# Small SBUF tiles of a diffusion-trunk kernel widened to whole 512-byte lines

## The chip, the cores and the metric

The kernel runs on one core of a Trainium2 chip. The number that counts is the device time of one execution in microseconds (us); several executions are timed and the median is taken. One more execution is recorded by the hardware profiler, and all that is said of single instructions comes from that one.

A core has a tensor engine (PE) that multiplies matrices, a vector engine (DVE), a scalar engine (ACT), GpSimd (POOL), a queue engine that issues most transfers (SP), and 16 DMA engines. The on-chip memory SBUF has 128 partitions; a tile occupies the same range of bytes in every partition. A matrix product has two operands in SBUF. The *stationary* one (here 128 columns, 512 bytes in each partition) is loaded into the array by an instruction of its own, which the profile lists as PEld. The *moving* one (here mostly 512 columns, 2048 bytes in each partition) is then streamed past it, and the sums land in PSUM. In the profile's names, `out<-moving,stationary`.

## What is computed

Two layers of a trunk over 256 latent and 256 context tokens of width 1024, in float32. Layer 0 is a convolution module, layer 1 a retention over chunks; each is followed by a gated feed-forward net of hidden width 2816, and each sub-layer is normalised and modulated by vectors made from a condition.

```python
for i in range(DEPTH):                      # DEPTH = 2
    sh_m, sc_m, g_m, sh_f, sc_f, g_f = adaln(c, ada_w[i], ada_b[i])
    hx = modulate(x, norm_mix[i], sh_m, sc_m)
    ...
    ox = conv_module(...) if i == 0 else retention_mixer(...)
    x = x + g_m * ox
    x = x + g_f * swiglu_ffn(modulate(x, norm_ffn[i], sh_f, sc_f), ffn_w_gu[i], ffn_w_down[i])
    if not last:                            # the context passes through layer 0 alone
        h_ctx = h_ctx + cg_m * oc
        h_ctx = h_ctx + cg_f * swiglu_ffn(modulate(h_ctx, ...), ffn_w_gu[i], ffn_w_down[i])
return x
```

## The kernel before

**Products in three passes.** Every large product is made by `mm3` (L188 to L192). Each operand is split into a high part and a low part of a 32-bit format that the tensor engine takes in one pass, and `hi*hi`, `hi*lo` and `lo*hi` are summed in PSUM. So all large products are runs of matmuls on lines L190, L191 and L192, 128 stationary columns by 512 (in a few places 256) moving columns. There are 4392 of them: 3912 with 512 moving columns and 480 with 256.

**Weights.** `load` (L141) brings 1 MB of weights by DMA into a `raw` tile, `split_hi` (L146) makes the high part on ACT (L153), `split_lo` (L157) the low part on DVE or POOL (L161). Three `raw` tiles and four pairs `wh`/`wl` take turns, so that loads and splits run ahead of the products.

**Stages in order of time.** Up to about 230 us: the modulation vectors of layer 0 (`ada`), the pointwise products of the convolution (`a`, `g` with `w1a`, `w1b` as stationary operand), the depthwise convolution, whose input takes a way through DRAM (`y` to `yd` to `z4`), and the last product `w`. 230 to 600 us: the feed-forward net of layer 0, up (`fa`, `fb`) and down (`dn`, `dnl`), while DVE works out the modulation of layer 1 (L850). 600 to 905 us: retention by heads (`qk`, `kc`, `v`, `sc`, `g` with `wg`, `o`, `wo`). From 905 us: the feed-forward net of layer 1, up (`u`) and down (`y`). The order of most instructions is pinned by hand; a scheduler orders the rest from a cost model.

**Which operand is which.** In `a`, `g` (w1b), `fa`, `fb` and `kc` the moving operand is the activation and the stationary one the weight. In `w`, `dn`, `dnl`, `qk`, `v`, `g` (wg), `wo`, `u` and `y` it is the other way round. In `o` the moving operand is the values and the stationary one the scores.

**Where tiles lie.** Pools are laid one behind the other in SBUF, and in a pool each tile follows the one declared ahead of it; the size in a partition is rounded up to 32 bytes and to nothing larger. The first tile starts at byte 16,512. Adding up the declared sizes gives the start of each tile, and so its remainder to 512 bytes. `cp` takes 21,440 bytes (among them `sm` with 1728, `cst` with 1168, `res`, the `mods` and `modA` tiles, `csil`, and `ab1` with 32), so that the weights and all that follows begin at 37,952 = 74 x 512 + 64. The small tiles of `sp` (`ss`, `rs_a`, `rstd`, `rs_h`, `rs_t`, two of 32 bytes each) add 320 bytes, `gcs` adds 2 x 64, and the tiles `lg` and `t8` of `rt` add 160.

| tiles (pool) | what they are to the tensor engine | start, remainder to 512, before |
|---|---|---|
| `wh`, `wl` (`wp`) | all split weights | 64 |
| `ah`, `al` (`pA`): `h0`, `z`, `hid`, `oT` | activations of `a`, `g`, `w`, `dn`, `wo` | 64 |
| `ah`, `al` (`pB`): `h0f`, `h1`, `h1f` | activations of `fa`, `fb`, `qk`, `v`, `kc`, `g`, `u` | 0 |
| `kT`, `qT`, `vh`, `vl` (`rt`); `hidT` in `kT`'s place | `sc`, values of `o`, activations of `y`, a few weights | 160 |
| `k4` (`sp`): `Ph`, `Pl` | scores of `o` | 384 |
| `idle` in `z4`'s place (`cv`) | both operands of the opening matmuls | 0 |
| `cst`, `csil` | identity and mean columns; the condition | 384; 32 |

All slices that the large products take out of these tiles begin at whole multiples of 512 bytes, so the remainder of the tile is that of every operand. Sorted by (moving, stationary), the 3912 wide ones are: (0, 64) `fa`, `fb`; (64, 0) `u`, `v`, `qk`, `g` with `wg`; (64, 160) `y`; (160, other) `o` and 48 matmuls with weights in `vh` and `vl`; (64, 64) `a`, `g` with `w1`, `w`, `dn`, `dnl`, `wo`.

Of the kernel before, what the change touches and what calls it, by code (L numbers as in the profile page):

```python
# [8 lines left out]
F32 = mybir.dt.float32  # L9
# [6 lines left out]
P = 128  # L16
D = 1024
KC = D // P
# [10 lines left out]
CST_W = 292  # L29
# [29 lines left out]
Z4 = 2  # L59
WSPLIT = 4  # L60
K4 = 5
YW = TOK + 2 * PAD
# [21 lines left out]
def trunk_kernel(ctx: ExitStack, tc, x_in, ctx_in, cond, small, consts, rope, dist, ada, adat,  # L84
# [3 lines left out]
    cp = ctx.enter_context(tc.tile_pool(name="cp", bufs=1))  # L88
    wp = ctx.enter_context(tc.tile_pool(name="wp", bufs=3))
    pA = ctx.enter_context(tc.tile_pool(name="pA", bufs=1))  # L90
    sp = ctx.enter_context(tc.tile_pool(name="sp", bufs=2))
# [3 lines left out]
    cv = cvs.enter_context(tc.tile_pool(name="cv", bufs=1))  # L95
# [4 lines left out]
    def aux(name):  # L100
        return ps.tile([P, 512], F32, tag="aux", name=name, bufs=2)
# [7 lines left out]
    nc.scalar.activation(tabl, one, AF.Silu)  # L109
    sm = cp.tile([P, SMALL_W], F32, name="sm")  # L110
    nc.scalar.dma_start(sm[:, 0:SMALL_1], small[:, 0:SMALL_1])
    cst = cp.tile([P, CST_W], F32, name="cst")
    nc.scalar.dma_start(cst, consts)
    ident = cst[:, 0:128]
    sel = cst[:, 128:130]
# [4 lines left out]
    def smc(n):  # L120
        a, b = _SM[n]
        return sm[:, a:b]
# [6 lines left out]

    load_tokens(x_in, 0)  # L130

    mods = [cp.tile([P, 48, 2], F32, name=f"mods{l}") for l in range(2)]
    modA = [[cp.tile([P, KC, 2], F32, name=f"modA{l}{j}") for j in range(2)] for l in range(2)]
    ab = smc("ab").rearrange("p (l c) -> p l c", l=2)
    ng = smc("ng").rearrange("p (l c) -> p l c", l=4)

    csil = cp.tile([P, KC, 32], F32, name="csil")
    nc.gpsimd.memset(csil, 0.0)


# [53 lines left out]
    def rsqrt(a, y, n, also=lambda i: None):  # L194


        nh = sp.tile([P, n], F32, tag="rs_h", name="rs_h")
        tt = sp.tile([P, n], F32, tag="rs_t", name="rs_t")
        also(nc.vector.tensor_scalar(y.bitcast(I32), a.bitcast(I32), -0.5, 1597463007.0, op0=ALU.mult, op1=ALU.add))
        also(nc.vector.tensor_scalar(nh, a, -0.5, None, op0=ALU.mult))  # L200
        for _ in range(3):
            for i in range(n):
                yi, ti = y[:, i:i + 1], tt[:, i:i + 1]
                also(nc.vector.tensor_scalar(ti, yi, yi, nh[:, i:i + 1], op0=ALU.mult, op1=ALU.mult))
            for i in range(n):
                yi, ti = y[:, i:i + 1], tt[:, i:i + 1]
                also(nc.vector.tensor_scalar(yi, ti, 1.5, yi, op0=ALU.add, op1=ALU.mult))

    def halves(t):
        return [t[:, 1024 * hf:1024 * hf + 1024].rearrange("p (k c) -> p k c", c=256) for hf in range(2)]  # L210
# [59 lines left out]
    def gate_to_rows(l, j, also=lambda i: None):  # L270

        c = 16 if j == 0 else 40
        pt = aux(f"gr{l}{j}")
        cs = sp.tile([P, 2, KC], F32, tag="gcs", name="gcs")
        also(nc.scalar.activation(cs, mods[l][:, c:c + KC, :].rearrange("p c s -> p s c"), AF.Copy))
        also(nc.tensor.transpose(pt[0:16, 0:P], cs.rearrange("p s c -> p (s c)"), ident))
        sb = sp.tile([16, P], F32, tag="grow", name="grow")
        also(nc.scalar.activation(sb, pt[0:16, 0:P], AF.Copy))
        d = dr.tile([2, D], F32, name=f"grd{l}{j}")
        also(nc.sync.dma_start(d.rearrange("s (c p) -> (s c) p", p=P), sb))  # L280
        gate_rows[l, j] = d
# [7 lines left out]
    def normed(tiles, xt=None, also=lambda i: None):  # L289

        n = len(tiles)
        outs = [xt[:, i, :] if xt is not None else sp.tile([P, D], F32, tag="k4", name="xn", bufs=K4)
                for i in range(n)]
        ss = sp.tile([P, n], F32, tag="ss", name="ss")
        for i, t in enumerate(tiles):
            also(nc.scalar.activation(outs[i], res[:, t, :], AF.Square, accum_out=ss[:, i:i + 1]))
        a = sp.tile([P, n], F32, tag="rs_a", name="rs_a")
        rstd = sp.tile([P, n], F32, tag="rstd", name="rstd")
        also(nc.vector.tensor_scalar(a, ss, 1.0 / D, EPS, op0=ALU.mult, op1=ALU.add))
        rsqrt(a, rstd, n, also)  # L300
        for i, t in enumerate(tiles):
            also(nc.vector.tensor_scalar(outs[i], res[:, t, :], rstd[:, i:i + 1], None, op0=ALU.mult))
        return outs
# [5 lines left out]
    def t2(name):  # L309
        return sp.tile([P, 512], F32, tag="t2", name=name, bufs=T2)  # L310
# [106 lines left out]
    start_loads("a0 w0 a1 w1 a2 w2")  # L417
    pin(nc.sync.dma_start(sm[:, SMALL_1:], small[:, SMALL_1:]))

    idle = cv.tile([P, 4, 2 * YW], F32, tag="z4", name="idle", bufs=Z4).rearrange("p q t -> p (q t)")[:, 0:512]  # L420
    nc.gpsimd.memset(idle, 0.0)
    pw_ = acc("idle")

# [4 lines left out]
    keep_busy(START_IDLE)  # L428
    xs = normed([0, 1], xn4[:, 0:2, :], pin)
    pin(nc.scalar.activation(csil[:, :, 0:2], smc("cT").rearrange("p (k c) -> p k c", c=2), AF.Silu))  # L430
    ab1 = cp.tile([P, KC], F32, name="ab1")
    pin(nc.vector.tensor_scalar(ab1, ab[:, 0, KC:2 * KC], 1.0, None, op0=ALU.add))
    xs += normed([2, 3], xn4[:, 2:4, :], pin)
    start_T(0, (0, 1))
# [30 lines left out]
        return sg.rearrange("p (s t) -> p s t", s=2)  # L465

    def glu(ch, pa, sg):
        y = cv.tile([P, 2, YW], F32, tag="y", name="y", bufs=4)
        nc.gpsimd.memset(y[:, :, 0:PAD], 0.0)
        nc.gpsimd.memset(y[:, :, PAD + TOK:], 0.0)  # L470
        yv = y[:, :, PAD:PAD + TOK]
        av = pa.rearrange("p (s t) -> p s t", s=2)
        if ch in GLU_DVE:
            pin(nc.vector.scalar_tensor_tensor(yv, av, b1[:, ch:ch + 1], sg, op0=ALU.add, op1=ALU.mult))
        else:
            pin(nc.scalar.activation(yv, av, AF.Identity, bias=b1[:, ch:ch + 1]))
            pin(nc.gpsimd.tensor_tensor(yv, yv, sg, op=ALU.mult))
        return y
# [7 lines left out]
    def bounce_in(ch, yd):  # L486

        n = GROUPS[ch]
        dg = cv.tile([P, MAXG, 4, 32], F32, tag="dg", name="dg", bufs=2)
        pin(nc.sync.dma_start(dg[:, :n], dwd[:, ch, :n]))  # L490
        z4 = cv.tile([P, 4, 2 * YW], F32, tag="z4", name="z4", bufs=Z4)
        w = 2 * YW - 3
        for s in range(4):
            pin(nc.sync.dma_start(z4[32 * s:32 * s + 32, :, 0:w], yd[:, :, s:s + w].rearrange("q c t -> c q t")))
        return z4, dg
# [134 lines left out]
    for step in range(KC):  # L630
        d = step - 1
        c = max(step - 2, 0) if step > 1 else None
# [23 lines left out]
        if step < KC - 1:  # L656
            ys[step] = glu(step, pa, sg)
            if step == 0:
                w1_hi(K_PAIRS + 1)
            if step:  # L660
                w1_load(step + W1_AHEAD)
            if step > 1 and step + 2 < KC:
                w1_hi(step + 2)
            zs4[step] = bounce_in(step, bounce_out(step, ys[step]))
# [24 lines left out]
        if step >= KC - 3:  # L689
            i = 2 * (step - KC + 3)  # L690
            square(i)
            square(i + 1)
        if step == KC - 1:
            split_w2(0, 0, None, pin)
            ys[step] = glu(step, pa, sg)
            pin(nc.scalar.activation(tabl, one, AF.Silu))
            zs4[step] = bounce_in(step, bounce_out(step, ys[step]))

    c, d = KC - 2, KC - 1
# [14 lines left out]
    for i in range(12, 16):  # L714
        t = fills[(i - 12) // 2][:, 2048 * (i % 2):2048 * (i % 2) + 2048]
# [1 line left out]
        ada_raws[i] = halves(t)  # L717
    w2r[0, 1] = load(w2[0, 1], name="w2_01", also=pin)
    for i in (16, 17):
        t = cv.tile([P, 4, 2 * YW], F32, tag="z4", name=f"raw_ada{i}", bufs=Z4).rearrange("p q t -> p (q t)")[:, 0:2048]  # L720
        pin(nc.sync.dma_start(t, ada[ADA_PE.index(i)]))
        ada_raws[i] = halves(t)
    cols(8)
# [37 lines left out]
    cols(13)  # L761
    finish(13)
    gate_to_rows(0, 0, pin)
    gates = [gate_bc(0, 0, 0, pin), gate_bc(0, 0, 1, pin)]
    ada_raws[18] = ada_load(18, pin)
# [143 lines left out]
    for gi, (j0, gn) in enumerate(groups):  # L909
        hid = new_act(pA, f"hid{gi}")  # L910
        for j in range(j0, j0 + gn):
# [14 lines left out]
            for j, w, pa, pb in early:  # L926
                sa = t2("sa")
                nc.scalar.activation(sa, pa, AF.Silu)
                t = t2("hidt")
# [3 lines left out]
        if gates is None:  # L933
            gate_to_rows(0, 1)
            gates = [gate_bc(0, 1, 0), gate_bc(0, 1, 1)]
# [45 lines left out]
    rt = ctx.enter_context(tc.tile_pool(name="rt", bufs=1))  # L981
    Wd = pA.tile([P, HEADS, 4, TOK], F32, tag="al", name="Wd")
    dec = smc("dec")
    lg = rt.tile([P, 8], F32, name="lg")

    def decay_logs():
        t8 = [rt.tile([P, 8], F32, name=f"t8_{i}") for i in range(4)]
# [78 lines left out]
    for hd in range(HEADS):  # L1066
# [5 lines left out]
        if hd == 0:  # L1072
            w = [kview(weights(wqk[0, kh], name=f"qk0{kh}", eng=nc.gpsimd if kh in QK_POOL else None), 512) for kh in range(2)]
            for kh in range(2):
                parts = norm_parts(1, 0, 1, x1, h, TOK, pin, pin if PIN_SPLIT else (lambda i: None)) if kh else None
                proj_half(qk_x, w[kh], kh, parts)
            for _ in parts:
                pass
            gate_to_rows(1, 0)
            gate_to_rows(1, 1)  # L1080
            qn = rope_q(pq, pin)
            for kh in range(2):
                keys_c(pk, w[kh], kh)
        else:
            for kh in range(2):
                w = kview(weights(wqk[hd, kh], name=f"qk{hd}{kh}"), 512)
                proj_half(qk_x, w, kh)
                keys_c(pk, w, kh)
# [358 lines left out]
```

## Time and profile before

| | us |
|---|---|
| median of 3 timed runs | 1097.86 |
| lowest and highest of them | 1094.61 and 1098.99 |
| the profiled execution | 1095.0 |
| its span, first to last instruction | 1093.2 |

The profiled execution lies 2.9 us below the median of the three runs and inside their spread. Outside its span lie 1.8 us.

How to read it: the profile's page gives busy time by engine and the chain of work that ended last; the timeline gives the start of every instruction. The duration that the timeline shows for a matmul includes its way through the array, which overlaps with the next one. What a matmul costs in a stream is therefore the time from one start to the next, and that is called its *pitch* below. It is taken from the first and the last row of a stretch without interruption, divided by the number of starts between them.

### The profile page before, as it was taken

How to read it: one execution, taken by the hardware profiler on the slowest of the kernel's cores; microseconds unless marked ns; L12 is line 12 of the kernel's file. 1: busy time of each engine (PE TensorE's matmuls, PEld its weight loads, DVE VectorE, ACT ScalarE, POOL GpSimd, SP SyncE). 2: the span in 40 equal slices, each digit the busy share in tenths (PEclk: the TensorE clock that was granted, in tenths of full speed). 3: DMA queues.
4: the chain of work that ended last, by engine and by line, in shares of the span. 5: the costliest groups of instructions: out<-in, count | busy, mean ns of one | idle time of the engine just before them, and what ended most of it. 6: DMA issues, size and time to landing. Idle time of an engine off the chain costs nothing.

```text
span 1093.2 us, 13554 instructions
## 1 busy us (share of the span) xinstructions
PE 1068.4 (98%) x5348; PEld 845.6 (77%) x5348; DVE 688.3 (63%) x1129; ACT 414.6 (38%) x596; POOL 162.2 (15%) x121
## 2 busy tenths in 40 slices
PE   8989998999999999999999999999999989999998
PEld 4756645788888888888888788888888867888886
DVE  5598765568999885536555786457454555555445
ACT  4564544353221222212322573323332454444442
POOL 0086743030000000000000420000000461000000
PEclk9999999999999999999999999999999999999999
DMA  9489778723556676523222442235233344455551
GB/s 375 178 231 274 233 195 349 264 78 116 211 213 243 258 269 231 172 98 133 98 81 112 158 152 92 101 135 178 92 116 116 116 161 166 167 181 191 192 187 45
DMA packets 34895, 190.15 MB, mean 174 GB/s; under 512 B 3920, under 2 KB 4624, under 8 KB 15504
## 3 DMA queue, kind: packets, MB, share of 16 engines
q1 hardware_dynamic: 34400, 188.01, 48.8%
q10 hardware_dynamic: 432, 1.28, 0.4%
q8 instruction: 42, 0.69, 0.3%
q14 instruction: 21, 0.17, 0.1%
HBM read 185.85 MB, written 3.42 MB: 173 GB/s over the span
## 4 chain that ended last, share of the span: by engine, by line
PE 88%; DMA 3%; DVE 3%; ACT 2%; issue 1%; POOL 1%; SPq 0%; ACTq 0%; POOLq 0%; DVEq 0%
PE fa L191 4%; PE fa L192 4%; PE fb L191 4%; PE fb L192 4%; PE fa L190 4%; PE fb L190 4%; PE u L190 3%; PE u L192 3%; PE u L191 3%; PE v L191 3%; PE v L192 3%; PE v L190 3%; PE dn L191 3%; PE dn L192 3%; PE dn L190 3%; PE g L192 2%
## 5 line engine op out<-in xcount | busy, mean ns | idle before, releaser
L161 DVE TENSOR_TENSOR wl_gu<-raw_gu,wh_gu 128x1024 fp32r<-128x1024 f32 x76 | 92.2, 1223 | 82.3 <-ACT wh_gu L153 81.4
L153 ACT ACTIVATE wh_gu<-raw_gu 128x1024 fp32r<-128x1024 f32 x84 | 88.0, 1058 | 139.6 <-PE fb L191 52.6
L850 DVE SCALAR_TENSOR_TENSOR junk<-raw_adat,crow 128x1024 f32<-128x1024 f32 x80 | 97.6, 1220 | 0.9
L161 DVE TENSOR_TENSOR wl_dn<-raw_dn,wh_dn 128x1024 fp32r<-128x1024 f32 x38 | 46.5, 1224 | 45.4 <-ACT wh_dn L153 45.1
L190 PE MATMUL fa<-ah_h0f,wh_gu 128*128 128x512 f32 (+1 forms) x192 | 72.0, 376 | 1.0 <-DVE ah_h0f L314 1.0
L191 PE MATMUL fa<-al_h0f,wh_gu 128*128 128x512 f32 (+1 forms) x192 | 72.3, 377 | 0.0
L190 PE MATMUL fb<-ah_h0f,wh_gu 128*128 128x512 f32 (+1 forms) x192 | 72.2, 376 | 0.0
L191 PE MATMUL fb<-al_h0f,wh_gu 128*128 128x512 f32 (+1 forms) x192 | 72.0, 375 | 0.0
L192 PE MATMUL fb<-ah_h0f,wl_gu 128*128 128x512 f32 (+1 forms) x192 | 72.0, 375 | 0.0
L192 PE MATMUL fa<-ah_h0f,wl_gu 128*128 128x512 f32 (+1 forms) x192 | 72.0, 375 | 0.0
L153 ACT ACTIVATE wh_dn<-raw_dn 128x1024 fp32r<-128x1024 f32 x38 | 40.3, 1060 | 80.3 <-PE dn L192 35.5
L190 PE MATMUL u<-wh_gu,ah_h1f 128*128 128x512 f32 x160 | 63.5, 397 | 0.0
L161 POOL TENSOR_TENSOR wl_qk<-raw_qk,wh_qk 128x1024 fp32r<-128x1024 f32 x4 | 9.6, 2398 | 362.7 <-DVE res L345 350.2
L191 PE MATMUL u<-wl_gu,ah_h1f 128*128 128x512 f32 x160 | 62.6, 392 | 0.0
L192 PE MATMUL u<-wh_gu,al_h1f 128*128 128x512 f32 x160 | 62.4, 391 | 0.0
L520 POOL TENSOR_TENSOR pacc<-pacc,pr 128x512 f32<-128x512 f32 x39 | 58.7, 1506 | 15.8 <-ACT pr L519 13.4
L537 DVE SCALAR_TENSOR_TENSOR lacc<-y,sm,lacc 128x512 f32<-128x512 f32 x65 | 49.1, 755 | 2.1
L191 PE MATMUL v<-wl_v,ah_h 128*128 128x512 f32 x128 | 50.4, 393 | 0.0
L192 PE MATMUL v<-wh_v,al_h 128*128 128x512 f32 x128 | 50.1, 391 | 0.0
L190 PE MATMUL dn<-wh_dn,ah_hid 128*128 128x512 f32 x128 | 49.9, 390 | 0.0
L191 PE MATMUL dn<-wl_dn,ah_hid 128*128 128x512 f32 x128 | 49.8, 389 | 0.0
L192 PE MATMUL dn<-wh_dn,al_hid 128*128 128x512 f32 x128 | 49.8, 389 | 0.0
(309 smaller groups left out, 2653.0 us busy)
## 6 DMA issues: line engine op xcount, KB each, us to landing
raw_gu<-in_gu_dram SPq DMA_DIRECT2D x44, 1024.0 KB, 4.8
raw_adat<-in_adat_dram SPq DMA_DIRECT2D x28, 1024.0 KB, 4.8
raw_dn<-in_dn_dram SPq DMA_DIRECT2D x19, 1024.0 KB, 4.7
raw_ada<-in_ada_dram SPq DMA_DIRECT2D x13, 1024.0 KB, 9.2
z<-yd SPq DMA_DIRECT2D x32, 284.5 KB, 4.8
raw_qk<-in_wqk_dram SPq DMA_DIRECT2D x8, 1024.0 KB, 4.8
raw_v<-in_wv_dram SPq DMA_DIRECT2D x8, 1024.0 KB, 4.8
raw_g<-in_wg_dram SPq DMA_DIRECT2D x8, 1024.0 KB, 4.8
```

Of the source, the lines that this page charges most:

```text
L153: also(nc.scalar.activation(hi[:, :m], raw[:, c:c + m], AF.Copy))
L161: also((eng or nc.vector).tensor_tensor(lo[:, :m], raw[:, c:c + m], hi[:, :m].bitcast(F32), op=ALU.subtract))
L190: also(nc.tensor.matmul(o, a[0], b[0], start=first, stop=False))
L191: also(nc.tensor.matmul(o, a[0], b[1], start=False, stop=False))
L192: also(nc.tensor.matmul(o, a[1], b[0], start=False, stop=last))
L520: pin(nc.gpsimd.tensor_tensor(pacc, pacc, pr, op=ALU.add))
L537: pin(nc.vector.scalar_tensor_tensor(cacc, a, w, cacc, op0=ALU.mult, op1=ALU.add))
L850: pin(nc.vector.scalar_tensor_tensor(junk, raw[:, c, :], 1.0, crow[:, s, :], op0=ALU.mult, op1=ALU.mult, accum_out=mods[l][:, c0 + c, s:s ...
```

## The change

No instruction is added, removed or changed in shape. Some small tiles are declared wider and then cut to the part in use, and some are declared at an earlier place.

```diff
+    mods = [cp.tile([P, 48, 2], F32, name=f"mods{l}") for l in range(2)]
+    modA = [[cp.tile([P, KC, 2], F32, name=f"modA{l}{j}") for j in range(2)] for l in range(2)]
+
+    ab1 = cp.tile([P, 32], F32, name="ab1")[:, 0:KC]
+    csil = cp.tile([P, KC, 32], F32, name="csil")
-    cst = cp.tile([P, CST_W], F32, name="cst")
+    cst = cp.tile([P, 384], F32, name="cst")[:, 0:CST_W]
...
-        tt = sp.tile([P, n], F32, tag="rs_t", name="rs_t")
+        tt = sp.tile([P, 32], F32, tag="rs_t", name="rs_t")[:, 0:n]
...
-        cs = sp.tile([P, 2, KC], F32, tag="gcs", name="gcs")
+        cs = sp.tile([P, 64], F32, tag="gcs", name="gcs")[:, 0:2 * KC].rearrange("p (s c) -> p s c", s=2)
...
-    idle = cv.tile([P, 4, 2 * YW], F32, tag="z4", name="idle", bufs=Z4).rearrange("p q t -> p (q t)")[:, 0:512]
+    idle = cv.tile([P, 2304], F32, tag="z4", name="idle", bufs=Z4)[:, 0:512]
...
-        y = cv.tile([P, 2, YW], F32, tag="y", name="y", bufs=4)
+        y = cv.tile([P, 576], F32, tag="y", name="y", bufs=4)[:, 0:2 * YW].rearrange("p (s t) -> p s t", s=2)
...
-        z4 = cv.tile([P, 4, 2 * YW], F32, tag="z4", name="z4", bufs=Z4)
+        z4 = cv.tile([P, 2304], F32, tag="z4", name="z4", bufs=Z4)[:, 0:8 * YW].rearrange("p (q t) -> p q t", q=4)
...
-        t = cv.tile([P, 4, 2 * YW], F32, tag="z4", name=f"raw_ada{i}", bufs=Z4).rearrange("p q t -> p (q t)")[:, 0:2048]
+        t = cv.tile([P, 2304], F32, tag="z4", name=f"raw_ada{i}", bufs=Z4)[:, 0:2048]
...
-    lg = rt.tile([P, 8], F32, name="lg")
+    lg = rt.tile([P, 96], F32, name="lg")[:, 0:8]
```

Added up in the same way, `cp` takes 21,888 bytes, so that the weights begin at 38,400 = 75 x 512; the small tiles of `sp` take 512 bytes, `gcs` 2 x 256, `lg` and `t8` together 512. Every tile of the table above then begins at a multiple of 512, `cst` and `csil` too, and `k4`. The pool of the convolution ends 1152 bytes later than before, and all still fits. Inside `z4` the rows of 2288 bytes stay as they were, and of the four `y` tiles (2304 bytes each) two begin in the middle of a line.

More of the change, by code (lines that the diff above doesn't have):

```diff
@@ L130, in trunk_kernel @@
     load_tokens(x_in, 0)
-    mods = [cp.tile([P, 48, 2], F32, name=f"mods{l}") for l in range(2)]
-    modA = [[cp.tile([P, KC, 2], F32, name=f"modA{l}{j}") for j in range(2)] for l in range(2)]
     ab = smc("ab").rearrange("p (l c) -> p l c", l=2)
     ng = smc("ng").rearrange("p (l c) -> p l c", l=4)
-    csil = cp.tile([P, KC, 32], F32, name="csil")
     nc.gpsimd.memset(csil, 0.0)
@@ L430, in trunk_kernel @@
     pin(nc.scalar.activation(csil[:, :, 0:2], smc("cT").rearrange("p (k c) -> p k c", c=2), AF.Silu))
-    ab1 = cp.tile([P, KC], F32, name="ab1")
     pin(nc.vector.tensor_scalar(ab1, ab[:, 0, KC:2 * KC], 1.0, None, op0=ALU.add))
```

## The prediction

> **What bounds the kernel now.** The page comes first: busy time by engine, granted clock, and the chain that ended last.
>
> ```profile
> span 1093.2 us, 13554 instructions
> ...
> PE 1068.4 (98%) x5348; PEld 845.6 (77%) x5348; DVE 688.3 (63%) x1129; ACT 414.6 (38%) x596; POOL 162.2 (15%) x121
> ...
> PEclk9999999999999999999999999999999999999999
> ...
> PE 88%; DMA 3%; DVE 3%; ACT 2%; issue 1%; POOL 1%; SPq 0%; ACTq 0%; POOLq 0%; DVEq 0%
> ```
>
> PE is busy for 98% of the span at full clock, and 88% of the chain is its own work. The busy time by stretches says where.
>
> ```profile
> 230.00:600.00 370.00, 368.10 (x1699) 302.40 (x1698) 258.27 (x449) 96.48 (x116) 9.35 (x4) 1.00 0.47 171
> 600.00:905.00 305.00, 299.33 (x1492) 250.08 (x1492) 180.22 (x318) 128.77 (x184) 59.85 (x29) 1.00 0.36 130
> 905.00:1084.00 179.00, 178.46 (x800) 144.62 (x799) 90.31 (x99) 76.69 (x101) 1.50 (x1) 1.00 0.45 162
> ```
>
> The columns are the length, then PE, PEld, DVE, ACT and POOL busy with their instructions, clock and DMA. From 230 us on PE has 8.1 us without work in 854 us, and DVE, the next engine, is busy for 70% at most. So a nanosecond less between two matmuls is nearly a nanosecond less in the time, once for each.
>
> The third view is the timeline of PE. Here are the first and the last row of one stretch in each family; between the rows lie 56, 24, 18, 12, 5 and 5 starts.
>
> ```profile
> 469.83 0.39 PE L191 MATMUL dn<-wl_dn,ah_hid 128*128 128x512 f32 x1
> ...
> 482.52 0.39 PE L190 MATMUL dn<-wh_dn,ah_hid 128*128 128x512 f32 x1
> ```
> ```profile
> 425.78 0.39 PE L190 MATMUL fa<-ah_h0f,wh_gu 128*128 128x512 f32 x1
> ...
> 431.38 0.39 PE L190 MATMUL fb<-ah_h0f,wh_gu 128*128 128x512 f32 x1
> ```
> ```profile
> 87.68 0.39 PE L190 MATMUL g<-ah_h,wh_w1b 128*128 128x512 f32 x1
> ...
> 91.77 0.39 PE L190 MATMUL g<-ah_h,wh_w1b 128*128 128x512 f32 x1
> ```
> ```profile
> 980.82 0.39 PE L190 MATMUL u<-wh_gu,ah_h1f 128*128 128x512 f32 x1
> ...
> 983.57 0.39 PE L190 MATMUL u<-wh_gu,ah_h1f 128*128 128x512 f32 x1
> ```
> ```profile
> 978.49 0.40 PE L190 MATMUL y<-wh_dn,hidT 128*128 128x512 f32 x1
> ...
> 979.66 0.40 PE L192 MATMUL y<-wh_dn,hidT 128*128 128x512 f32 x1
> ```
> ```profile
> 667.00 0.40 PE L192 MATMUL o<-vh,Pl 128*128 128x512 f32 x1
> ...
> 668.16 0.39 PE L192 MATMUL o<-vh,Pl 128*128 128x512 f32 x1
> ```
>
> The pitch of one and the same form is 226.6 ns in `dn` (12.69 us / 56), 233.3 in `fa` (5.60 / 24), 227.2 in `g` with w1b (4.09 / 18), 229.2 in `u` (2.75 / 12), 234 in `y` (1.17 / 5) and 232 in `o` (1.16 / 5). What sets these apart? Not the role of the operands: `g` and `fa` both stream activations past weights, with 227.2 and 233.3. Not the stage: `dn` and `fa` take turns in the same 370 us. The table of starts fits: 227 where both operands have the remainder 64, more wherever the two differ: 229 at (64, 0), 233 at (0, 64), 234 at (64, 160), 232 at (160, 384).
>
> **The change part by part.** The program stays the same instruction for instruction; all that moves is addresses. So the sum is one of pitches times counts. After the change every large product has (0, 0), a pair that no wide one has now. I take it that two operands with the same remainder run at the pitch of `dn`, 226.6, since (64, 64) is the one alike pair that the trace has at this width.
>
> The counts, one line of three for each family (three passes, so three times as many; `qk`, `g`, `dnl`, `wo` follow from the loops):
>
> ```profile
> L190 PE MATMUL u<-wh_gu,ah_h1f 128*128 128x512 f32 x160 | 63.5, 397 | 0.0
> L191 PE MATMUL fa<-al_h0f,wh_gu 128*128 128x512 f32 x160 | 63.1, 394 | 0.0
> L190 PE MATMUL fb<-ah_h0f,wh_gu 128*128 128x512 f32 x160 | 63.1, 394 | 0.0
> L190 PE MATMUL v<-wh_v,ah_h 128*128 128x512 f32 x128 | 49.6, 390 | 0.0
> L190 PE MATMUL y<-wh_dn,hidT 128*128 128x512 f32 x88 | 33.1, 396 | 0.0
> L190 PE MATMUL o<-vh,Ph 128*128 128x512 f32 x32 | 12.6, 395 | 0.0
> ```
>
> *`fa`, `fb`:* 960 x (233.3 - 226.6) = 6.4 us. *`u`, `v`, `qk`, `g` with wg:* 1272 x (229.2 - 226.6) = 3.3 us at most. These stages are broken up by transposes. An alike stream needs a few matmuls after such a break: in `wo`, also (64, 64), the ten starts below take 2.29 us, 229 each.
>
> ```profile
> 737.04 0.39 PE L191 MATMUL wo<-wl_wo,oT 128*128 128x512 f32 x1
> ...
> 739.33 0.39 PE L192 MATMUL wo<-wh_wo,oT 128*128 128x512 f32 x1
> ```
>
> So I take 1272 x 1.6 = 2.0 us (the bounds are 0, if all behave like this stretch, and 3.3). *`y`:* 264 x (234 - 227.5) = 1.7 us. *`o` and the 48 with weights in `vh`, `vl`:* 144 x (232 - 227) = 0.7 us. The gross gain is 10.8 us.
>
> The 480 matmuls with 256 columns may lose. The one alike pair among them is `sc`, (160, 160); `fa` and `fb` of the first two blocks have (0, 64). Between these rows lie 18 and 12 starts.
>
> ```profile
> 656.62 0.28 PE L190 MATMUL sc<-qT,kT 128*128 128x256 f32 x1
> ...
> 658.78 0.28 PE L190 MATMUL sc<-qT,kT 128*128 128x256 f32 x1
> ```
> ```profile
> 239.58 0.28 PE L190 MATMUL fa<-ah_h0f,wh_gu 128*128 128x256 f32 x1
> ...
> 240.94 0.28 PE L190 MATMUL fa<-ah_h0f,wh_gu 128*128 128x256 f32 x1
> ```
>
> `sc` has 120 ns, `fa` 113.3 at its best. `sc` and `dn` together say that 256 more columns cost 226.6 - 120 = 106.6 ns, so 512 stream in 213.2, and an alike matmul adds 13.4 at either width (`fa`: 20.1 at 512, but 6.7 at 256). The bounds are 384 x 6.7 = 2.6 us lost (`kc` and `fa`/`fb` all go from 113.3 to 120) and 96 x 6.7 = 0.6 us gained (`sc` goes to 113.3). I take 1.7 us lost, two thirds of the way to the upper end, because `sc` is the only row with an alike pair.
>
> The other engines see moved addresses too. The nearest rows set two remainders side by side:
>
> ```profile
> L850 DVE SCALAR_TENSOR_TENSOR junk<-raw_adat,crow 128x1024 f32<-128x1024 f32 x80 | 97.6, 1220 | 0.9
> L161 DVE TENSOR_TENSOR wl_gu<-raw_gu,wh_gu 128x1024 fp32r<-128x1024 f32 x76 | 92.2, 1223 | 82.3 <-ACT wh_gu L153 81.4
> ...
> raw_gu<-in_gu_dram SPq DMA_DIRECT2D x44, 1024.0 KB, 4.8
> raw_adat<-in_adat_dram SPq DMA_DIRECT2D x28, 1024.0 KB, 4.8
> ```
>
> `raw_adat`, `crow` and `junk` begin at remainder 0, `raw_gu` and `wh_gu` at 64; DVE takes 1220 and 1223 ns and the transfer lands after 4.8 us in both. I count DVE, ACT, POOL and DMA at nothing. Nothing hides them at the bounce `y` to `yd` to `z4`, but the rows there keep their 2288 bytes. The single-pass products of the first 230 us (`ada`, depthwise `cv`, transposes) I also count at nothing, with 1 us to either side.
>
> One stretch of the chain is not PE's:
>
> ```profile
> 871.75 4.77 POOL wo301vl L161 x2
> 876.53 4.65 DMA raw_gu<-in_gu_dram
> ```
>
> From 870 to 905 us a faster PE only waits longer for these; the 48 matmuls with weights in `vh` and `vl` lie there and save nothing: 48 x 5 ns, 0.3 us with their neighbours. What is late next is DVE in 300 to 400 us, where it also makes the modulation of layer 1; the row of 230 to 600 us (258 of 370 busy) leaves room for 3%. **Sum:** 10.8 - 1.7 - 0.3 = 8.8 us. From the profiled execution's 1095.0 that makes 1086.2; the median of the runs lies 2.9 us higher, so **1089**.
>
> **The rivals.** The whole is 3912 x (pitch after - mean pitch now), and the mean now is 230.1 ns (960 x 233.3, 1272 x 229.2, 1272 x 227.5, 264 x 234, 144 x 232).
>
> *Slower: a moving operand at remainder 0 is what costs.* `fa`, `fb` are the only wide family that has it, and among the slowest. Then all go to 233.3: 3912 x 3.2 = 12.5 us more, 1110. It decides from 230.1 ns on. Against it: `fa` with 256 columns also moves from 0 and adds only 6.7 ns, half of `sc`; and the opening matmuls on `idle` have (0, 0).
>
> ```profile
> 7.24 4.03 PE L426 MATMUL idle<-idle 128*128 128x512 f32 x9
> ```
> ```profile
> L426 PE MATMUL idle<-idle 128*128 128x512 f32 x7 | 3.2, 593 | 0.0
> ```
>
> Nine of them end 4.03 us after the first start, so the pitch is (4.03 - 0.59) / 8 = 430 ns; that is twice 213.2 and 3 ns. They stream at half the rate, so this is a hint, not a proof.
>
> *Little or nothing.* Either (0, 0) behaves like (64, 0): 3912 x (229.2 - 230.1) is 3.5 us less, and 1.7 come back at 256 columns: 1096. Or the remainder is not the cause: 1098. For this speaks only that the pairs coincide with families; `dn` beside `fa` and `g` beside `fa` speak against. The Trainium skill, TensorE: Matmul & The Clock Gate, section "Step-by-step: what each phase is for", states that PE reads its two operands through independent ports and that a load of the next weights takes nothing from the running matmul; by that rule placement could not matter and the time would stay. The rows from 226.6 to 234 do not agree with it.
>
> *Much faster: the 13.4 ns go as well.* If what `idle` shows holds at full rate, the pitch is 216: 3912 x 14 = 55 us less, 1043. Against it: `dn` at 226.6 and `sc` at 120 are alike already and pay 13.4. The Trainium skill, TensorE: Matmul & The Clock Gate, section "Wait — 56ns, not 53.3ns?", gives 215.7 ns for 512 columns back to back; by it the gain would be 56 us, an estimate from that page. The rows of `dn` do not agree with it.
>
> **How the numbers follow.** Alike pairs as with (64, 64): 0.66, between 1083 and 1094, from the ends of the terms (gross 8.8 to 12.5, loss 2.6 to gain 0.6, 1 us for the start, and the spread of the runs). Little or nothing: 0.17. Slower: 0.13. Much faster: 0.04. Such runs can tell about 0.5%, 5.5 us, from no change. Of the first case a tenth falls within that: faster 0.62 + 0.04 = 0.66; within 0.5% 0.20; slower 0.14, with a little from the scatter of the others. The range 1081 to 1100 takes in the first two cases and leaves the two outer ones out.
>
> **What would show it.** Right: `fa`, `y`, `u` and `dn` all show one pitch near 227 in the timeline, the stretch 230 to 600 us is 6 us shorter and the start up to 230 us keeps its length. Wrong: `dn` goes up to 229 or 233 (the remainder itself counts, not the likeness), or `fa` stays at 233. If the pitches fall and the time does not, DVE or a load has become the wait, which PE's busy share would tell.

## The result, and the profile after

| | before | after |
|---|---|---|
| median of 4 timed runs, us | 1096.65 | 1086.38 |
| lowest and highest, us | 1094.61, 1098.99 | 1085.50, 1087.92 |
| the profiled execution, us (its span) | 1095.0 (1093.2) | 1087.21 (1085.4) |

The ratio is 0.9907, with a 95% interval of 0.9881 to 0.9934: the changed kernel is 0.9% faster, 10.3 us by the medians. PE, DVE, ACT and POOL have the same instructions in the same order in both traces (the one more that the page counts below belongs to the sequencer of POOL and is not counted as busy). In the changed kernel the three lines of `mm3` are L192 to L194, and later lines move down by one or two.

The page of the changed kernel: span, busy time, the granted clock in 40 slices, and the chain.

```profile
span 1085.4 us, 13555 instructions
...
PE 1062.3 (98%) x5348; PEld 851.1 (78%) x5348; DVE 687.8 (63%) x1129; ACT 414.9 (38%) x596; POOL 162.1 (15%) x121
...
PEclk8999999999999999999999999999999999999999
...
PE 91%; DVE 3%; DMA 2%; ACT 2%; issue 1%; SPq 0%; POOL 0%; ACTq 0%; DVEq 0%; POOLq 0%
```

PE is as much the bound as before. It is busy for 6.1 us less, and the span is 7.8 us shorter. DVE, ACT and POOL keep their time, and so do the rows that stood for moved addresses:

```profile
L163 DVE TENSOR_TENSOR wl_gu<-raw_gu,wh_gu 128x1024 fp32r<-128x1024 f32 x76 | 92.2, 1223 | 78.6 <-ACT wh_gu L155 77.8
...
L851 DVE SCALAR_TENSOR_TENSOR junk<-raw_adat,crow 128x1024 f32<-128x1024 f32 x80 | 97.7, 1221 | 0.9
...
raw_gu<-in_gu_dram SPq DMA_DIRECT2D x44, 1024.0 KB, 4.7
raw_adat<-in_adat_dram SPq DMA_DIRECT2D x28, 1024.0 KB, 4.8
```

Where the time went is read from the same instructions in both traces. The view of one tile gives, for each line, the count, the shortest, median and longest duration in ns, and the first and last start in us. Before:

```profile
L190 PE MATMUL fa<-ah_h0f,wh_gu x192: 276/394/398, 231.1 to 563.8; 128*128 128x512 f32 x160, 128*128 128x256 f32 x32
L192 PE MATMUL dnl<-wh_dn_l,al_hid x48: 389/389/400, 570.6 to 605.7; 128*128 128x512 f32 x48
L192 PE MATMUL wo<-wh_wo,oT x56: 387/389/398, 724.0 to 894.7; 128*128 128x512 f32 x56
L190 PE MATMUL y<-wh_dn,hidT x88: 391/394/481, 919.4 to 1087.4; 128*128 128x512 f32 x88
```

After:

```profile
L192 PE MATMUL fa<-ah_h0f,wh_gu x192: 277/389/396, 232.6 to 559.9; 128*128 128x512 f32 x160, 128*128 128x256 f32 x32
L194 PE MATMUL dnl<-wh_dn_l,al_hid x48: 389/389/397, 566.4 to 601.5; 128*128 128x512 f32 x48
L194 PE MATMUL wo<-wh_wo,oT x56: 388/390/397, 719.4 to 889.0; 128*128 128x512 f32 x56
L192 PE MATMUL y<-wh_dn,hidT x88: 389/390/477, 914.4 to 1080.0; 128*128 128x512 f32 x88
```

The first `fa` starts 1.5 us *later* than before (232.6 against 231.1). The last `dnl` starts 4.2 us earlier, so the feed-forward net of layer 0 gained 5.7 us. By the last `wo` the lead is 5.7 us (1.5 more), by the first `y` 5.0, and by the last `y` 7.4 (2.4 more). The two places where the lead shrinks, before 231 us and between 889 and 914 us, hold stretches at half clock, shown in the last section.

The pitches, from the timeline of PE after, first and last row of a stretch. From the first row to the last it is 48 starts (`dn`), 23 (`fa`), 46 (`u`), 13 (`y`), 23 (`o`) and 24 (256 columns):

```profile
457.18 0.39 PE L192 MATMUL dn<-wh_dn,ah_hid 128*128 128x512 f32 x1
...
468.06 0.39 PE L192 MATMUL dn<-wh_dn,ah_hid 128*128 128x512 f32 x1
```
```profile
272.06 0.39 PE L192 MATMUL fa<-ah_h0f,wh_gu 128*128 128x512 f32 x1
...
277.28 0.39 PE L194 MATMUL fa<-ah_h0f,wl_gu 128*128 128x512 f32 x1
```
```profile
957.62 0.39 PE L193 MATMUL u<-wl_gu,ah_h1f 128*128 128x512 f32 x1
...
968.07 0.39 PE L194 MATMUL u<-wh_gu,al_h1f 128*128 128x512 f32 x1
```
```profile
934.64 0.39 PE L192 MATMUL y<-wh_dn,hidT 128*128 128x512 f32 x1
...
937.59 0.39 PE L193 MATMUL y<-wl_dn,hidT 128*128 128x512 f32 x1
```
```profile
858.77 0.39 PE L192 MATMUL o<-vh,Ph 128*128 128x512 f32 x1
...
863.98 0.39 PE L194 MATMUL o<-vh,Pl 128*128 128x512 f32 x1
```
```profile
240.96 0.28 PE L194 MATMUL fb<-ah_h0f,wl_gu 128*128 128x256 f32 x1
...
243.84 0.28 PE L194 MATMUL fa<-ah_h0f,wl_gu 128*128 128x256 f32 x1
```

`dn` has 226.7 ns (10.88 us / 48), `fa` 227 (5.22 / 23), `u` 227.2 (10.45 / 46), `y` 226.9 (2.95 / 13), `o` 226.5 (5.21 / 23). The families that lay between 226.6 and 234 ns now share one pitch. `fa` with 256 columns went the other way, from 113.3 to 120 (2.88 / 24).

### The profile page after: what moved, and what is told of

Read it like the earlier page. It is cut to its first block, busy times and chain, and to the rows that moved or that the text cites. A ratio compares the mean times of both kernels' runs of the same rounds, so it can differ in the third digit from the quotient of the medians.

```text
span 1085.4 us, 13555 instructions
## 1 busy us (share of the span) xinstructions
PE 1062.3 (98%) x5348; PEld 851.1 (78%) x5348; DVE 687.8 (63%) x1129; ACT 414.9 (38%) x596; POOL 162.1 (15%) x121
## 3 DMA queue, kind: packets, MB, share of 16 engines
HBM read 185.85 MB, written 3.42 MB: 174 GB/s over the span
## 4 chain that ended last, share of the span: by engine, by line
PE 91%; DVE 3%; DMA 2%; ACT 2%; issue 1%; SPq 0%; POOL 0%; ACTq 0%; DVEq 0%; POOLq 0%
PE u L194 4%; PE fa L193 4%; PE u L193 4%; PE u L192 4%; PE fa L194 4%; PE fb L194 4%; PE fa L192 4%; PE fb L193 4%; PE fb L192 4%; PE v L193 3%; PE v L192 3%; PE dn L192 3%; PE dn L194 3%; PE v L194 3%; PE dn L193 3%; PE g L192 2%
## 5 line engine op out<-in xcount | busy, mean ns | idle before, releaser
L192 PE MATMUL fa<-ah_h0f,wh_gu 128*128 128x512 f32 (+1 forms) x192 | 71.4, 373 | 1.0 <-DVE ah_h0f L316 1.0
L192 PE MATMUL fb<-ah_h0f,wh_gu 128*128 128x512 f32 (+1 forms) x192 | 71.5, 373 | 0.0
L194 PE MATMUL fb<-ah_h0f,wl_gu 128*128 128x512 f32 (+1 forms) x192 | 71.4, 372 | 0.0
L194 PE MATMUL fa<-ah_h0f,wl_gu 128*128 128x512 f32 (+1 forms) x192 | 71.3, 372 | 0.0
L192 PE MATMUL u<-wh_gu,ah_h1f 128*128 128x512 f32 x160 | 63.1, 394 | 0.0
L194 PE MATMUL u<-wh_gu,al_h1f 128*128 128x512 f32 x160 | 62.3, 391 | 0.0
L521 POOL TENSOR_TENSOR pacc<-pacc,pr 128x512 f32<-128x512 f32 x39 | 58.7, 1505 | 15.7 <-ACT pr L520 13.4
L192 PE MATMUL dn<-wh_dn,ah_hid 128*128 128x512 f32 x128 | 49.9, 390 | 0.0
L194 PE MATMUL v<-wh_v,al_h 128*128 128x512 f32 x128 | 49.9, 390 | 0.0
L194 PE MATMUL dn<-wh_dn,al_hid 128*128 128x512 f32 x128 | 49.8, 389 | 0.0
```

Source lines behind the costliest of these rows:

```text
L192: also(nc.tensor.matmul(o, a[0], b[0], start=first, stop=False))
L194: also(nc.tensor.matmul(o, a[1], b[0], start=False, stop=last))
L521: pin(nc.gpsimd.tensor_tensor(pacc, pacc, pr, op=ALU.add))
```

## The experiments

In all of them only the place of tiles is varied. Diffs are against the changed kernel unless the text says otherwise. Let *d* be the start of the stationary operand less that of the moving one, modulo 256 bytes. Before, `fa` has *d* = 64, `u`, `v`, `qk` 192, `y` 96, `dn` 0.

**The change itself, timed once more.**

> The change as it is, timed again beside the three variants of this call. Both theories: 1086 us, 0.990 of before, one pitch of 227 ns in all wide products.

1087.26 us (6 runs) against 1095.84 (17): ratio 0.9916 [0.9898, 0.9935].

**Whole lines without likeness, and likeness without whole lines.** The first kernel keeps the edits of `cp`, `idle`, `y` and `z4` and drops those of `rs_t`, `gcs` and `lg`: the weights and `pA` begin at whole lines, `pB` and `rt` don't.

```diff
-        tt = sp.tile([P, 32], F32, tag="rs_t", name="rs_t")[:, 0:n]
+        tt = sp.tile([P, n], F32, tag="rs_t", name="rs_t")
...
-        cs = sp.tile([P, 64], F32, tag="gcs", name="gcs")[:, 0:2 * KC].rearrange("p (s c) -> p s c", s=2)
+        cs = sp.tile([P, 2, KC], F32, tag="gcs", name="gcs")
...
-    lg = rt.tile([P, 96], F32, name="lg")[:, 0:8]
+    lg = rt.tile([P, 8], F32, name="lg")
```

> Only the first part of the change (mods, modA, ab1, csil, cst): weights and the activations of pA begin at remainder 0, the activations of pB at 448, rt at 96, k4 at 320. Theory 'likeness' (only the difference of the two starts counts, stationary minus moving, to 512): fa, fb have +64 and stay at 233 ns, u, v, qk have -64 and stay at 229, y has +96 and stays at 234, dn stays at 227; 1096.6 us, ratio 1.000. Theory 'line starts' (an operand costs less if it begins on a multiple of 512): the weights, and with them one operand of every product, now begin there, so fa, u and y fall by part of what the whole change gave, some 3 to 6 us; ratio 0.995.

The second is its counterpart: the change without the edit of `cp` (`mods`, `modA`, `ab1`, `csil`, `cst` as before). All operands lie alike at 64.

> All of the change but its first part: weights, activations, k4 and rt all begin at remainder 64, cst stays at 384 and csil at 32. Likeness: one pitch of 227 ns everywhere and 120 ns at 256 columns, as after the whole change; 1086.4 us, ratio 0.990. Line starts: no operand begins on a multiple of 512, so nothing is better than dn was before, and fa and u keep 229 or more; ratio 0.997 to 1.000.

The third moves everything to remainder 32 by eight floats.

```diff
-    ab1 = cp.tile([P, 32], F32, name="ab1")[:, 0:KC]
+    ab1 = cp.tile([P, 40], F32, name="ab1")[:, 0:KC]
```

> The change with ab1 32 bytes wider, so that every operand, cst and csil too, begins at remainder 32. Likeness: 227 ns everywhere, 1086.4 us, ratio 0.990. Line starts: every operand lies across lines, 229 to 234 ns everywhere, 1093 us or more, ratio 0.997 to 1.012.

| kernel | us | ratio to before |
|---|---|---|
| without the edits of `rs_t`, `gcs`, `lg` | 1095.74 (12 runs) | 0.9993 [0.9982, 1.0004] |
| all but the edit of `cp` (all at 64) | 1087.76 (6) | 0.9917 [0.9899, 0.9935] |
| all at 32 | 1087.30 (6) | 0.9916 [0.9898, 0.9935] |

The timeline shows why. Without the edits of `rs_t`, `gcs` and `lg`, 23 and 46 starts apart:

```profile
271.35 0.39 PE L192 MATMUL fa<-ah_h0f,wh_gu 128*128 128x512 f32 x1
...
276.71 0.40 PE L194 MATMUL fa<-ah_h0f,wl_gu 128*128 128x512 f32 x1
...
965.16 0.39 PE L193 MATMUL u<-wl_gu,ah_h1f 128*128 128x512 f32 x1
...
975.70 0.39 PE L194 MATMUL u<-wh_gu,al_h1f 128*128 128x512 f32 x1
```

With all at 32, 23 starts apart:

```profile
269.82 0.39 PE L192 MATMUL fa<-ah_h0f,wh_gu 128*128 128x512 f32 x1
...
275.03 0.39 PE L194 MATMUL fa<-ah_h0f,wl_gu 128*128 128x512 f32 x1
```

Weights on whole lines against activations that aren't: `fa` 233 (5.36 / 23) and `u` 229.1 (10.54 / 46), as before. No operand on a whole line, but all alike: 226.5. At 512 columns the remainder itself, tried at 0, 32 and 64, is of no account; the likeness is.

**Other distances.** Three kernels put pads ahead of `ah_h0` in `pA`, in `sp`, and ahead of `qT`, and widen `lg`, so that the families stand at distances that before didn't have. The pads (in floats, `pA`, `sp`, `qT`, and `lg`) are 32, 32, 32, 168 in the first, 8, 40, 64, 104 in the second, 16, 72, 112, 208 in the third. The first as a diff:

```diff
+        if (l, j) == (0, 0):
+            sp.tile([P, 32], F32, name="padB", bufs=1)
...
+    pA.tile([P, 32], F32, name="padA")
...
-    lg = rt.tile([P, 96], F32, name="lg")[:, 0:8]
+    lg = rt.tile([P, 168], F32, name="lg")[:, 0:8]
...
+        rt.tile([P, 32], F32, tag="padQ", name="padQ", bufs=1)
```

> After the change, with unused tiles put in so that pA begins at remainder 128, pB at 256, kT, vh, vl at 32, qT at 160; weights at 0. Differences (stationary minus moving): a, g -128; w, dn, dnl, wo +128; fa, fb -256; u, v, qk +256; y +32; o +96; sc -128. Likeness to 512 bytes: none is alike, so 229 to 234 ns in all wide products, some 7 to 12 us more than the changed kernel, 1094 to 1098 us. Likeness to 256 bytes: fa, fb, u, v, qk stay at 227 and only the rest rises; 1088 to 1090 us. Likeness to 128 bytes: all but y and o stay at 227; 1087 us.

> As offsets_1, with pA at 32, pB at 192, kT, vh, vl at 224, qT at 480. Differences: a, g -32; w, dn, dnl, wo +32; fa, fb -192; u, v, qk +192; y +224; o -192; sc -256. Likeness to 512, 256 or 128 bytes: none is alike, 229 to 234 ns everywhere, 1094 to 1098 us. If the price grows with the distance, dn and a at 32 are below fa and u at 192.

> As offsets_1, with pA at 64, pB at 352, kT, vh, vl at 288, qT at 224. Differences: a, g -64; w, dn, dnl, wo +64; fa, fb +160; u, v, qk -160; y -224; o -224; sc +64. Likeness: the roles swap prices against the kernel before: a, g at 229 ns (as u had it at -64), w, dn at 233 (as fa had it at +64), u near 234 as the pair (160, 0) had it; 1094 to 1098 us. If instead the role of the operand set the price, a, g would go with fa at 233 and dn with u at 229.

One run each: 1093.15, 1103.12 and 1107.92 us, with the kernel before at 1097.6 on the same chip. In the first, `fa` and `u` have operands 256 apart, `dn` 128 (23, 46 and 48 starts apart):

```profile
271.46 0.39 PE L192 MATMUL fa<-ah_h0f,wh_gu 128*128 128x512 f32 x1
...
276.68 0.39 PE L194 MATMUL fa<-ah_h0f,wl_gu 128*128 128x512 f32 x1
...
457.65 0.40 PE L192 MATMUL dn<-wh_dn,ah_hid 128*128 128x512 f32 x1
...
468.80 0.40 PE L192 MATMUL dn<-wh_dn,ah_hid 128*128 128x512 f32 x1
...
962.70 0.40 PE L193 MATMUL u<-wl_gu,ah_h1f 128*128 128x512 f32 x1
...
973.14 0.40 PE L194 MATMUL u<-wh_gu,al_h1f 128*128 128x512 f32 x1
```

`fa` 227 (5.22 / 23) and `u` 227 (10.44 / 46): half a line apart costs nothing, so the period is 256 bytes, not 512. `dn` 232.3 (11.15 / 48). In the second kernel `dn` is only 32 bytes apart (23 starts):

```profile
465.42 0.40 PE L192 MATMUL dn<-wh_dn,ah_hid 128*128 128x512 f32 x1
...
470.77 0.40 PE L194 MATMUL dn<-wh_dn,al_hid 128*128 128x512 f32 x1
```

That is 232.6 (5.35 / 23), no better than 128. The price does not grow with the distance. In this kernel `fa` and `u` stand at -192 and +192, and their means are 233.3 and 229.5: those of before, where they stood at +64 and -64, which is the same modulo 256. In the third kernel `g` with w1b, which streams activations past weights as `fa` does, has *d* = 192, and `u` 96 (20 and 46 starts apart):

```profile
87.75 0.39 PE L192 MATMUL g<-ah_h,wh_w1b 128*128 128x512 f32 x1
...
92.33 0.40 PE L194 MATMUL g<-ah_h,wl_w1b 128*128 128x512 f32 x1
...
975.12 0.39 PE L193 MATMUL u<-wl_gu,ah_h1f 128*128 128x512 f32 x1
...
985.88 0.39 PE L194 MATMUL u<-wh_gu,al_h1f 128*128 128x512 f32 x1
```

`g` now has 229 (4.58 / 20), the pitch that `u` had before; `u` has 233.9 (10.76 / 46), that of `y`. So the price goes by *d*, not by what the operands hold. Over all families of these kernels and of before, by the mean of the uninterrupted pitches:

| *d* (stationary less moving, modulo 256) | pitch, 512 columns, ns | seen in |
|---|---|---|
| 0 | 226.7 (`dn`, `fa`) to 227.7 (`u`, which transposes break up) | `dn`; `fa`, `u` after, and 256 apart |
| 192 | 229.1 to 229.5 | `u` before and in the second, `g` in the third |
| 32, 64, 96, 128, 160, 224 | 232.4 to 234 | `fa` (64), `y` (96), `dn` (128, 32), `fa` (160), `o` (224) |

The three times missed what I had expected. The pitches by themselves weren't to blame: in the first kernel the 1272 matmuls of the families of `dn`, `a` and `w` at *d* = 128 cost 5.7 ns each, 7.3 us in all, and I had left most of that out. Added up over all large products (up to 245 ns each), the pitches of the three kernels lie 8.2, 15.8 and 21.8 us above those of the changed kernel; by its median of 1086.38 the times lie 6.8, 16.7 and 21.5 us above.

**A shift of 64 bytes inside a stream.** The weights' low parts and, in `pA`, the activations' low parts lie 64 bytes off the high parts; `pB` and `rt` lie at 64 as a whole. The three passes of `mm3` then differ in *d*: 0, 192, 64 in `dn`, 64, 0, 64 in `u`, 192, 192, 0 in `fa`.

```diff
+            if name == "w1a0":
+                wp.tile([P, 16], F32, name="padW", bufs=1)
...
-    h = new_act(pA, "h0")
+    pA.tile([P, 48], F32, name="padA")
+    h0 = pA.tile([P, KC, 512], F32R, tag="ah", name="ah_h0")
+    pA.tile([P, 16], F32, name="padL")
+    h = (h0, pA.tile([P, KC, 512], F32R, tag="al", name="al_h0"))
```

> After the change, with unused tiles put in so that high and low parts lie apart: wh at remainder 0 to 256, wl at 64, ah of pA at 0, al of pA at 64, everything in pB and rt at 64. Two theories of which two operands meet. 'Own pair': moving and stationary operand of one matmul; then the three passes of w, dn, dnl have differences 0, -64 and +64 and pitches of 227, 229 and 233 (mean 229.7), and fa, fb have 229, 229, 227 in the order of their passes (hi hi, hi lo, lo hi). 'Next load': the moving operand of one matmul and the stationary operand of the next, which is loaded meanwhile; then w, dn, dnl and a, g with w1 have difference 0 in all three steps and 227 throughout, and fa, fb have 229, 227, 229. Both: u, v, qk 233, 227, 233, so the time is 6 to 9 us above the changed kernel's.

1102.97 us in one run: 16 us above the changed kernel, more than I had expected, and 15.3 by the sum of the pitches. The timeline, 23, 47 and 46 starts apart (the lines are L194 to L196 here):

```profile
275.01 0.39 PE L194 MATMUL fa<-ah_h0f,wh_gu 128*128 128x512 f32 x1
...
280.28 0.39 PE L196 MATMUL fa<-ah_h0f,wl_gu 128*128 128x512 f32 x1
...
462.35 0.39 PE L194 MATMUL dn<-wh_dn,ah_hid 128*128 128x512 f32 x1
...
473.22 0.39 PE L196 MATMUL dn<-wh_dn,al_hid 128*128 128x512 f32 x1
...
970.56 0.39 PE L195 MATMUL u<-wl_gu,ah_h1f 128*128 128x512 f32 x1
...
981.29 0.39 PE L196 MATMUL u<-wh_gu,al_h1f 128*128 128x512 f32 x1
```

By the table of *d* above, taken pass by pass, the means would be 228.4 (`fa`), 229.7 (`dn`) and 231.1 (`u`). Measured are 229.1 (5.27 / 23), 231.3 (10.87 / 47) and 233.3 (10.73 / 46): 0.7 to 2.2 more each. A matmul's price thus isn't set by its own pair alone, and pass by pass it is plainer still: in `u` the pass on L195, whose own pair is alike, has the highest mean, 235.0, against 234.2 and 230.2 on L194 and L196. That the moving operand meets the *next* weights doesn't fit either: in `dn` all three pairs would then be alike, at 227. Which reads meet stays open. What is shown: a shift inside a stream costs more than the single pairs do.

**Which edits carry the gain.** The kernel before, with the edits of `rs_t`, `gcs` and `lg` and none of the others.

> The kernel before with three lines of the change alone (rs_t, gcs, lg), so that weights, activations, k4 and rt all begin at remainder 64; cst, csil, idle, y and z4 as before. Likeness: the whole gain, 227 ns everywhere, ratio 0.991 to 0.992. If the widened cst, csil or z4 carried a part, that part is missing: ratio 0.994 or more.

1086.83 us (6 runs), ratio 0.9919 [0.9900, 0.9937]: all of it. The edits of `cp`, `idle`, `y` and `z4` carry nothing that can be measured. The same with `sc` set to *d* = 64 by a pad, since 256 columns ran best there:

```diff
+        rt.tile([P, 48], F32, tag="padQ", name="padQ", bufs=1)
```

> three_lines with qT 192 bytes further, so that sc alone has the difference +64, at which the narrow fa and sc took 113 to 115 ns instead of 120. Likeness: 96 x 6 ns = 0.6 us less than three_lines if these lie on the path, ratio 0.9910 against 0.9916, which is at the edge of what the runs can tell; the pitch of sc is 114.

1085.62 us (4 runs), ratio 0.9899 [0.9884, 0.9914]. The intervals overlap, and the pitch of `sc` came to 117.7, not to 114: 96 x 2 ns is 0.2 us, so the 1.2 us between the two medians aren't shown to come from it. The third of the kernels above has `sc` at *d* = 64 too, and there it took 114.7: at 256 columns *d* alone does not set the pitch, and what else does stays open.

## Why the prediction was right

**The rule.** "Two operands with the same remainder run at the pitch of `dn`" held: 226.5 to 227.2 in all the rows above, and again with all at 64 and all at 32 (`fa` 226.7 on average in both). The remainder to 512 was finer than needed; 256 sorts the families just as well, and the table's (0, 64) and (64, 0) were the two sides of one signed distance.

**The terms.** The third column adds up, over every pitch that nothing interrupts (up to 245 ns), what lies above 226.7 ns, or 115 at 256 columns, before less after.

| term | predicted, us | measured, us |
|---|---|---|
| `fa`, `fb` | 6.4 | 6.35 |
| `u`, `v`, `qk`, `g` | 2.0 | 2.2 (0.9, 0.7, 0.4, 0.2) |
| `y` | 1.7 | 1.4 |
| `o` and the 48 | 0.7 | 0.8 (0.6, 0.2) |
| 256 columns | -1.7 | -1.5 |

All families together come to 9.4 us; the sum on record was 8.8, with 0.3 taken off for the wait near 890 us, which pitches can't show. The choice between bounds for `u` and its like was right for the reason given: an alike stream needs some matmuls after each break. From 600 us on the first six pitches after one average 230 to 234 ns in the changed kernel, and 226.6 is reached at the eleventh. So the means over the whole stage are 227.1 (`v`) to 228.1 (`g`), not 226.7. The choice at 256 columns was right too: alike is not best there, and `fa` went to 120 as `sc` had.

**The sum and the time.** The profiled executions differ by 7.8 us, 1 less than the sum, the medians by 10.3, 1.5 more. The profiled execution after lost 1.5 us at the start and 0.7 near 893 us in the stretches at half clock. The one with all at 32 has no half clock near 16 to 22 us; its span is 9.6 us shorter than that of before, where its pitches give 9.1. 1086.38 lies 2.6 us under the forecast; nearly half of that (1.2) is the median of before, which came to 1096.65 in four runs where three had given 1097.86. The 2.9 us that were added from the profiled execution to the median were no property of the kernel: after, the profiled execution lies 0.8 us above its median.

**What was to show it.** One pitch for `fa`, `y`, `u` and `dn`: yes. 230 to 600 us shorter by 6: 5.7. "The start up to 230 us keeps its length": no, it took 1.5 us longer in the profiled execution. That step failed for a reason outside the sum, the clock, not for the single-pass products: with all at 32, without the half clock near 16 to 22 us, the first `fa` starts at 230.4 us, 0.8 earlier than before.

**The rivals.** *A moving operand at remainder 0 costs*: refuted by `fa` at 227 from 0, and `dn` at 226.7. *Little or nothing*: refuted by the interval and by the kernel with whole lines but unlike operands. This is also what the independent ports of the Trainium skill (TensorE: Matmul & The Clock Gate, section "Step-by-step: what each phase is for") would give; no kernel here agrees, since with the same instructions the pitch moves between 226.5 and 234 ns with the place of the operands alone. *Much faster*: refuted, no wide stream at full clock came below 226.5. Where the 13.4 ns above the streaming time come from is not shown by any run.

## What to carry to other kernels

Where PE is the bound and its matmuls follow each other without a gap, add up the starts of the tiles in a partition and compare stationary and moving operand modulo 256 bytes, high and low parts alike; three small tiles widened were enough here, and no tile has to begin on a whole line. Make the whole stream alike, since a shift between high and low parts cost more than the single pairs had said. Weigh the counts first: at 512 columns 2.5 to 7 ns of some 230 are to be had for each matmul, and at 256 columns likeness lost up to 6.7.

## What was not expected of the hardware

**The period and the sign.** 256 bytes apart costs nothing and 32 costs 6; *d* = 192 costs 2.5 ns where *d* = 64 costs 6.6.

**Half clock in the middle of the kernel.** The changed kernel, windows of 2 or 3 us (length, PE, PEld, DVE, ACT, POOL busy, clock, DMA share, GB/s):

```profile
18.00:20.00 2.00, 2.00 (x7) 1.71 (x7) 0.80 (x3) 0.93 (x2) 0.00 (x0) 0.50 1.05 445
...
890.00:893.00 3.00, 0.73 (x2) 0.30 (x2) 1.76 (x3) 1.55 (x3) 3.00 (x2) 0.99 0.94 330
893.00:896.00 3.00, 2.82 (x7) 2.24 (x8) 2.02 (x4) 2.00 (x3) 3.00 (x2) 0.50 0.98 411
```

Before, the same first stretch, and for the other two the windows with about the same work, which comes 5 to 6 us later there:

```profile
18.00:20.00 2.00, 1.94 (x8) 1.37 (x8) 0.83 (x3) 1.10 (x3) 0.00 (x0) 1.00 1.04 426
...
896.00:900.00 4.00, 1.89 (x7) 1.28 (x8) 3.09 (x5) 1.55 (x4) 4.00 (x3) 1.00 0.94 365
900.00:905.00 5.00, 5.00 (x24) 4.10 (x23) 2.66 (x11) 3.10 (x5) 5.00 (x3) 1.00 0.87 326
```

Eight matmuls of the changed kernel in and behind the first of its windows:

```profile
18.92 0.63 PE L193 MATMUL a<-al_h,wh_w1a 128*128 128x512 f32 x1
...
22.34 0.50 PE L192 MATMUL g<-ah_h,wh_w1a 128*128 128x512 f32 x1
```

Their pitch is 427.5 ns (3.42 us / 8), 201 more than 226.7: 1.6 us are lost in these eight alone, and the first `fa` was late by 1.5. It goes with the execution rather than with the placement: of the profiled executions with all operands alike, those of the change (both), of the kernel without the edit of `cp` and of the three lines have it, those with all at 32 (span 1083.6 us) and with the pad for `sc` (1084.6) don't; before doesn't either. The second kernel of the other distances has it without likeness in any wide family. And the change by itself seems to come with and without: of its ten timed runs five have a mean granted clock of 0.992 or 0.993, five of 0.996 or 0.997.

The one near 893 us lies between 890 and 900 us in all six executions with alike operands. It comes behind a wait: PE was busy for 0.73 of the 3.00 us ahead of it, and before for 1.89 of 4.00 us without losing the clock. From the last `wo` to the first `y` these six take 25.4 to 25.5 us, and the three executions without such a stretch (before, the third of the other distances, the shift by 64 bytes) 24.7 to 24.8. What sets either off was not tried. The Trainium skill, TensorE: Matmul & The Clock Gate, section "Part 1: The HAM clock gate (the "warmup" mystery)", says that a hardware monitor halves the clock by how busy PE has been. Ahead of the first stretch, from 14 to 16 us, PE was busy for 1.35 of 2.00 us before and for 1.45 in the changed kernel, and only the latter went to half clock, so this case shows the halving but not its rule.
